# A diffusion backbone layer on one core: where the second halves of the normed tokens are made before an expert layer

## The chip, the core and the metric

One core of a Trainium2 chip runs the whole layer in one launch. The metric is the device time in microseconds (us). The engines named here are TensorE (PE, with its weight loads as PEld), VectorE (DVE), ScalarE (ACT), GpSimd (POOL) and SyncE (SP, which issues the loads from memory). Each engine works off its own instruction stream in order, and waits for others by semaphores.

## What is computed

The layer norms 512 latent tokens of width 1024, mixes them (neighbourhood attention and an RWKV-7 scan), projects and adds them to the residual, norms again, and sends each token to two of 32 experts. Everything of the change lies around the second norm, the router and the start of the expert layer:

```python
    yx = jnp.concatenate([na_x, rw_x], axis=-1) @ w_out
    x = x + mod_x[2] * yx
    hx2 = modulate(rmsnorm(x, norm2_g[l]), mod_x[3], mod_x[4])
    ...
    g_logits = (hf @ wg + bg).astype(jnp.float32)
    g_sel = jnp.argmax(g_logits, axis=-1)
    ...
    top_v, top_i = lax.top_k(e_logits, MOE_TOPK)
    ...
    for e in range(N_EXPERTS):
        he = jax.nn.silu(hf @ w1[e]) * (hf @ w3[e])
        out = out + combine[:, e:e + 1] * (he @ w2[e])
```

Inputs and weights are fp32. Each expert has three matrices of 2 MB (w1, w3, w2), so that the 32 experts read 201 MB.

## The kernel before

The 512 tokens lie in four tiles of 128 tokens, worked in the order 3, 2, 1, 0. `out_end` does the last of the output projection (`proj_rw`, whose accumulators are `acc`), the norm of each tile (`norm2`: transposes `pt`, sums of squares by ACT into `st`, a reciprocal root in small DVE steps into `rs`), and the router's logits (`logits`: `plg`, then `lt`, `plt` and `lg`). `best` finds the chosen experts of two tiles in some thirty small DVE instructions; its mask for the slots is `chosen`. `best(2)` serves tiles 3 and 2, `best(0)` tiles 1 and 0.

Tokens are gathered for the experts by matmuls with one-hot matrices (`oh2t` for tiles 3 and 2, `OH` afterwards), into PSUM tiles `pga`. The normed tokens come in two fp32r halves, so that the products keep fp32's precision: `xh` is x times its scale, rounded, made by ACT, and `xl` is what the rounding left, made by POOL out of an unrounded copy `xn` and `xh`. `halves` is a generator that makes both for one tile: one step makes `xh`, each further step a copy `xn` of 512 columns and its `xl`. For tiles 1 and 0 the copies lie in the room of the features `HS` instead of in `xn`. After the gather of batch 0 (experts 0 to 3), ACT scales `pga` into `HS`, and the experts' matmuls `ph` (w1 and w3) and `py` (w2) follow, two experts at a time.

The experts' weights are 384 loads of 512 KB, `wt`, all issued by SP in the order of use, and gathered in a ring of 31 tiles: `RING = (6, 15, 3, 3, 2, 2)` tiles in six pools, wt0 to wt5. The loads start long before the expert layer. A tile of the ring is memory that earlier work used, so its first load waits for the last reader there; from the 32nd on a load waits for the matmuls that used the tile before. wt1 and wt5 are allocated on the right side of memory, over the room of the pool `PR`, in which the router's small tiles (`lg`, `cwr`, `chosen`, `tsb`, then `xn`, then the tiles of `best`) lie one after the other. The SP queue is in order, so a load that waits holds back all behind it.

In `moe_phase`, `route_b` turns `chosen` into places (`byt`, line `s.pp[:, 0:2]`), two `slots` make the one-hot matrices `OH`, the rest of `best(0)` makes the weights of the chosen experts, and `route_c` writes the other places (the last `byt`, and the last reader of `chosen`). The scheduler orders an engine's stream except where code pins an instruction (`s.pin`) or an engine is kept in program order.

Of the kernel before, what the change touches and what calls it, by code (L numbers as in the profile page):

```python
# [8 lines left out]
F32 = mybir.dt.float32  # L9
# [3 lines left out]
AF = mybir.ActivationFunctionType  # L13
ALU = mybir.AluOpType
# [169 lines left out]
FIRST = ('k0', 'r0', 'v0')  # L184
ITEMS = (('k1', 'r1', 'v1', 'nk0'), ('k2', 'r2', 'v2', 'nq0'), ('k3', 'r3', 'v3', 'nv0'), ('nk1', 'gd', 'nq1', 'nv1'))  
MODGAP = 3.43  
H1 = (3, 2, 0)
UPE = lambda nc: nc.vector
LAST = 16  
OUT_ORD = ('scalar',)  # L190
# [35 lines left out]
class K:  # L226
# [1207 lines left out]
    def out_end(s, PCs):  # L1434

        nc, tc, ctx = s.nc, s.tc, s.ctx
        xt = s.MIX.tile([128, 8, 256], F32, name="xnt0", tag="mA")
        s.norm2(3, xt, 0, 'ch')
        acc = [[s.ps(tag=t, name="acc") for t in tt] for tt in (('ip', 'ip'), ('nt', 'rm'))]
        for n, _ in enumerate(s.proj_rw((1,), acc[0:1])):  # L1440
            if n == 3:
                s.norm2(2, xt, 1, 'ch')
        s.finish_b(0)
        lt = s.logits(xt, 'ch')
        PCs.close()
        s.BE.close()
        s.psc.close()
        ctx.enter_context(s.psum_pool("psg", g=2, m=2))
        PX = ctx.enter_context(tc.tile_pool(name="pxa", bufs=1, side="right", reuse_waits="tile"))
        s.xl, s.xh = [[PX.tile([128, 1024], F32R, name=f"{n}{i}") if i > 1 else None for i in range(4)] for n in ("xl", "xh")]  # L1450
        s.RT = ExitStack()
        s.PR = s.RT.enter_context(tc.tile_pool(name="pr", bufs=1, side="right", reuse_waits="tile"))
        s.lg = s.PR.tile([128, 4, 36], F32, name="lg")
        s.cwr = s.PR.tile([128, 2, 32], F32, name="cwr")
        s.chosen = s.PR.tile([128, 5, 32], BF16, name="chosen")
        nc.gpsimd.memset(s.chosen[:, 0], 0.0)

        s.tsb = s.PR.tile([128, 256], BF16, name="tsb")
        nc.gpsimd.tensor_copy(s.tsb, s.tsf)
        s.nio = s.L.tile([128, 32], F32, name="nio")  # L1460
        nc.gpsimd.tensor_copy(s.nio, s.niof)
        xt = s.MIX.tile([128, 8, 256], F32, name="xnt1", tag="mA")
        s.ordered = OUT_ORD
        for n, _ in enumerate(s.proj_rw((0,), acc[1:2])):
            if n == 1:
                s.logits_end((3, 2), lt)
                h = s.halves(3)
                s.some(h, 2)
            if n == 3:
                s.norm2(1, xt, 0)  # L1470
                s.some(h, 2)
        s.all(s.best(2))
        h = s.halves(2)
        s.some(h, 2)
        s.norm2(0, xt, 1)
        oh = s.route_a()
        lt = s.logits(xt)
        begun = s.begun = [s.ps((128, 2, 256), tag=g, name="pga") for g in ('rm', 'nt')]
        early = [(b, z, i) for b in range(4) for i in (3, 2) for z in range(2)]
        for b, z, i in early[:EARLY]:  # L1480
            s.gather_tiles(begun[b], oh, b, z, (i,))
        s.some(h, 2)
        s.logits_end((1, 0), lt)
        begun += [s.ps((128, 2, 256), tag='g', name="pga") for _ in range(2)]
        for b, z, i in early[EARLY:]:
            s.gather_tiles(begun[b], oh, b, z, (i,))

        s.mod5 = [s.ps(tag='m', name="mod5") for _ in range(2)]
        for m, c in zip(s.mod5, s.COLS):
            s.mm(m, s.cst[0:1, C_IOTA:C_IOTA + 1].to_broadcast([1, 128]), s.grow[:, c])  # L1490
        s.strict = False

    def norm2(s, i, xt, z, tag='m'):

        nc, PO = s.nc, s.PO
        st = PO.tile([128, 4], F32, name="st2", bufs=2)
        jk = PO.tile([128, 512], BF16, name="jk2", bufs=2)
        x = s.x1[:, i]
        for b in range(2):
            c = s.COLS[b]  # L1500
            pt = s.ps(tag=tag, name="pt2")
            for k in range(4):
                s.tr(pt[:, 128 * k:128 * k + 128], x[:, 512 * b + 128 * k:512 * b + 128 * k + 128])
            o = xt[:, 4 * b:4 * b + 4, 128 * z:128 * z + 128]
            p4 = pt.rearrange("p (a b) -> p a b", b=128)
            if b:
                nc.vector.tensor_copy(o, p4)
            else:
                s.act(o, p4)
            s.act(jk, x[:, c], AF.Square, accum_out=st[:, b:b + 1])  # L1510
        nc.vector.tensor_tensor(st[:, 1:2], st[:, 0:1], st[:, 1:2], ALU.add)
        nc.vector.tensor_scalar(st[:, 1:2], st[:, 1:2], 1.0 / D, EPS, op0=ALU.mult, op1=ALU.add)
        s.rsqrt(s.rs2[:, i:i + 1], st[:, 1:2], st[:, 3:4])

    def halves(s, i, room=None):

        rs = s.rs2[:, i:i + 1]
        s.act(s.xh[i], s.x1[:, i], AF.Copy, scale=rs)
        for c in s.COLS:
            yield  # L1520
            xn = room[:, c] if room is not None else s.PR.tile([128, 512], F32, name="xn")
            s.act(xn, s.x1[:, i, c], AF.Copy, scale=rs)
            s.pin(s.nc.gpsimd.tensor_tensor(s.xl[i][:, c], xn, s.xh[i][:, c].bitcast(F32), ALU.subtract))

# [16 lines left out]
    def moe_phase(s):  # L1541
        tc, nc = s.tc, s.nc
        with ExitStack() as es:
# [20 lines left out]
            OH, HS = PM.tile([128, 4, 4, 64], F32R, name="OH"), s.features_room(PM)  # L1564

            f = HS.rearrange("p k n -> p (k n)")
            h1, h0 = s.halves(1, f[:, 0:1024]), s.halves(0, f[:, 1024:2048])
            for h, n in ((h1, H1[0]), (h0, H1[1]), (h1, 3), (h0, H1[2])):
                s.some(h, n)
            s.pin(nc.gpsimd.tensor_copy(s.cw[:, 2:4], s.cwr))  # L1570
            best = s.best(0, h0)
            next(best)
            s.dump('lg', s.lg)
            s.dump('x1', s.x1)
            s.route_b()
            for i in (1, 0):
                s.pin(s.slots(OH[:, i], s.pp[:, i, 0:4]))
            s.all(best)
            s.ordered = ()
            s.route_c()  # L1580
# [36 lines left out]
        nc.vector.tensor_tensor(oh, it, bc(ix), ALU.is_equal)  # L1617
        yield

    def best(s, i0, more=()):  # L1620

        nc, PO = s.nc, s.PR
        T = lambda n, *sh: PO.tile([128, *sh], F32, name=n)
# [6 lines left out]
        t4, z, pg = T("t4", 2, 4), T("z", 2), T("pg", 2)  # L1630
# [26 lines left out]
        ex, w1, w2 = T("ex", 8), T("w1", 8), T("w2", 8)  # L1657
        nc.vector.tensor_tensor(ex, m2, m1, ALU.subtract)
        s.act(ex, ex, AF.Exp)
        s.all(more)  # L1660
        nc.vector.tensor_scalar(w1, ex, 1.0, None, op0=ALU.add)
        nc.vector.reciprocal(w1, w1)
        nc.vector.tensor_tensor(w1, w1, f8(t4), ALU.mult)
# [68 lines left out]
        return s.nc.vector.tensor_tensor(out, s.cst[:, None, C_IOTA:C_IOTA + 64].to_broadcast([128, 4, 64]),  # L1732
                                  place[:, :, None].to_broadcast([128, 4, 64]), ALU.is_equal)

    def gather_tiles(s, pg, OH, b, z, tiles):

        c = slice(256 * b + 128 * z, 256 * b + 128 * z + 128)
        for i in tiles:
            r = OH[i].rearrange("p e n -> p (e n)")
            s.mm(pg[:, z], s.xh[i][:, c], r, i == 3 and z == 0, False)  # L1740
            s.mm(pg[:, z], s.xl[i][:, c], r, False, i == 0 and z == 1)

    def gather(s, OH, HS, begun=None):
        nc = s.nc
        for b in range(4):
            pg = begun[b] if begun else s.ps((128, 2, 256), tag='gm'[b % 2], name="pga")
            for z in range(2):
                s.gather_tiles(pg, [OH[:, i] for i in range(4)], b, z, (1, 0) if begun else (3, 2, 1, 0))
                if z == 0:
                    yield  # L1750
            for z in range(2):
                kt = 2 * b + z
                s.act(HS[:, kt], pg[:, z], AF.Identity, scale=s.sc2[:, kt:kt + 1], bias=s.modv[:, kt:kt + 1])
            yield
# [240 lines left out]
```

## Time and profile before

| | |
|---|---|
| median of 3 runs | 1197.58 us (1192.83 to 1199.34) |
| the profiled execution's own time | 1196.86 us |
| its span | 1195.1 us |
| busy share of the span: PE, PEld, DVE, ACT, POOL | 91%, 64%, 56%, 34%, 21% |
| DMA | 310 MB, mean 259 GB/s |

The span is what the profiler saw from the first to the last instruction; the own time is 1.76 us longer. Times in the rows below count from the span's start. A busy PE is not PE at its peak, since matmuls are pipelined.

### The profile page before, as it was taken

What the parts mean: (1) busy time and instruction counts of PE and PEld (TensorE: products, weight loads), DVE (VectorE), ACT (ScalarE), POOL (GpSimd) and SP (SyncE); (2) the same over time, 40 slices, a digit from 0 to 9 for tenths busy, and PEclk for the clock granted to TensorE, in tenths of its full rate; (3) what the DMA queues carried; (4) which work ended last, traced back from release to release, by engine and by line L of the source; (5) the groups of instructions that cost most, each with busy time, mean ns of one, the idle gap of its engine ahead of it and who ended that gap; (6) DMA issues with size and microseconds to landing.
All of it is one profiled execution on the core that took longest, in us unless ns stands there. A gap on an engine that the chain in (4) does not pass through costs nothing.

```text
span 1195.1 us, 23927 instructions
## 1 busy us (share of the span) xinstructions
PE 1090.3 (91%) x9673; PEld 760.0 (64%) x9674; DVE 664.2 (56%) x1445; ACT 400.5 (34%) x759; POOL 247.4 (21%) x277
## 2 busy tenths in 40 slices
PE   3899987897977888999988979999999999999996
PEld 1677776775855767888776754646464646464644
DVE  5645598798699624554478772333333333333335
ACT  3543543634645444555322251111111111120200
POOL 0654463353344300020253030000000000000000
PEclk9999987797997888999999989999999999999998
DMA  9534643545554477764353939999999999999995
GB/s 367 177 133 144 197 147 119 155 138 154 160 171 126 133 202 211 241 158 108 103 151 117 359 124 372 409 408 409 408 409 409 409 409 409 408 409 409 408 409 188
DMA packets 148765, 310.00 MB, mean 259 GB/s; under 512 B 32291, under 2 KB 71075, under 8 KB 148652
## 3 DMA queue, kind: packets, MB, share of 16 engines
q1 hardware_dynamic: 143868, 306.08, 71.9%
q10 hardware_dynamic: 4752, 2.36, 0.7%
q8 instruction: 77, 1.26, 0.4%
q14 instruction: 36, 0.29, 0.1%
q0 software_dynamic: 32, 0.00, 0.0%
HBM read 283.22 MB, written 25.17 MB: 258 GB/s over the span
## 4 chain that ended last, share of the span: by engine, by line
PE 55%; DVE 16%; DMA 6%; ACT 2%; issue 1%; POOL 1%; SPq 0%; DVEq 0%; POOLq 0%; ACTq 0%
PE ph L241 16%; PE py L241 9%; PE psc L241 7%; PE pga L241 5%; DMA wt<-in_w_dram 3%; DVE Tc L211 3%; DVE tmp L211 3%; PE pgr L241 3%; PE ipn L241 3%; PE pr L241 1%; PE ppt L245 1%; PE pon L241 1%; DVE fst L211 1%; DMA BKj<-BKd 1%; PE acc L241 1%
## 5 line engine op out<-in xcount | busy, mean ns | idle before, releaser
L241 PE MATMUL ph<-wt,HS 128*64 128x512 f32 x1024 | 224.5, 593 | 0.2 <-DMA wt<-in_w_dram 0.2
L241 PEld LDWEIGHTS ph<-wt,HS 128*64 128x64 f32 x1024 | 73.5, 137 | 140.5 <-issue 126.7
L211 DVE TENSOR_TENSOR hid<-hid,ph 128x512 f32<-128x512 f32 x16 | 11.0, 688 | 249.2 <-PE ph L241 249.2
L241 PE MATMUL py<-wt,hid 128*64 128x256 f32 x1024 | 114.5, 381 | 0.0
L241 PEld LDWEIGHTS py<-wt,hid 128*64 128x64 f32 x1024 | 71.9, 137 | 40.3 <-issue 3.9
L211 POOL CAST two<-sel 128x128 fp32r<-128x128 f32 x32 | 8.5, 293 | 425.3 <-PE pbc L241 425.3
L241 PE MATMUL ipn<-whi,hth 128*128 128x256 f32 x256 | 80.3, 314 | 15.8 <-DVE vs L211 15.3
L211 POOL TENSOR_TENSOR wlo<-wraw,whi 128x512 fp32r<-128x512 f32 x54 | 73.8, 1369 | 77.6 <-ACT whi L211 74.5
L211 DVE TENSOR_TENSOR x<-psc,x 128x512 f32<-128x512 f32 (+1 forms) x136 | 78.5, 648 | 0.0
L241 PE MATMUL ip<-hth,whi 128*128 128x512 f32 (+1 forms) x200 | 75.8, 379 | 1.9 <-ACT nr L211 1.9
L241 PE MATMUL ipn<-wlo,hth 128*128 128x256 f32 x256 | 75.6, 295 | 0.0
L241 PE MATMUL ipn<-whi,htl 128*128 128x256 f32 x256 | 75.4, 295 | 0.0
L241 PE MATMUL ip<-htl,whi 128*128 128x512 f32 (+1 forms) x200 | 72.2, 361 | 0.7 <-DVE htl L211 0.7
L241 PE MATMUL ip<-hth,wlo 128*128 128x512 f32 (+1 forms) x200 | 71.9, 359 | 0.0
L241 PEld LDWEIGHTS ipn<-whi,hth 128*128 128x128 f32 x256 | 51.9, 203 | 24.6 <-issue 22.1
L241 PE MATMUL pga<-OH,xh 128*128 128x256 f32 x240 | 60.0, 291 | 0.9 <-DVE OH L211 0.9
L211 DVE TENSOR_TENSOR Tc<-Tc,tmp 128x30 f32<-128x30 f32 (+14 forms) x120 | 59.4, 495 | 2.0
L211 DVE TENSOR_TENSOR tmp<-Mc,Tc 128x30 f32<-128x30 f32 (+14 forms) x120 | 57.7, 481 | 3.1 <-ACT Tc L211 1.1
L241 PE MATMUL pga<-OH,xl 128*128 128x256 f32 x240 | 59.0, 287 | 0.0
L241 PE MATMUL psc<-yh,oht 128*128 128x512 f32 (+1 forms) x136 | 54.5, 405 | 1.2 <-DVE x L211 0.8
L211 ACT ACTIVATE hid<-pth 128x512 f32<-128x512 f32 x16 | 9.6, 598 | 133.1 <-PE pth L245 133.1
L241 PEld LDWEIGHTS ipn<-whi,htl 128*128 128x128 f32 x256 | 52.3, 204 | 0.0
(352 smaller groups left out, 2252.6 us busy)
## 6 DMA issues: line engine op xcount, KB each, us to landing
wt<-in_w_dram SPq DMA_DIRECT2D x384, 512.0 KB
wm<-in_wmod_dram SPq DMA_DIRECT2D x48, 512.0 KB
wraw<-in_w_in_dram SPq DMA_DIRECT2D x30, 256.0 KB
wraw<-in_w_na_dram SPq DMA_DIRECT2D x24, 256.0 KB
BKj<-BKd SPq DMA_DIRECT2D x12, 512.0 KB
BKd<-BK SPq DMA_DIRECT2D x12, 384.0 KB
ARz<-ARd SPq DMA_DIRECT2D x16, 256.0 KB
wo<-in_w_out_dram SPq DMA_DIRECT2D x16, 256.0 KB
```

The lines of the kernel that those rows point to most:

```text
L211: i = f(*a, **k)
L241: i = s.nc.tensor.matmul(out, l, r, start=start, stop=stop)
L245: i = s.nc.tensor.transpose(out, x, s.ident if ident is None else ident)
```

## The change

It does four things. `halves` of tiles 3 and 2 run through at once, ahead of the norms of tiles 1 and 0, and `xn` gets two buffers (`XN = 2`). `halves` of tiles 1 and 0 make only `xh` and one whole copy early; their `xl` are four DVE subtractions behind the first two `OH`. Batch 0 gathers the `xh` of tiles 1 and 0 first and their `xl` last. In `norm2` the sum of squares stands ahead of the copy of the transposed tokens.

```diff
-H1 = (3, 2, 0)
+XN = 2
...
             if n == 1:
                 s.logits_end((3, 2), lt)
-                h = s.halves(3)
-                s.some(h, 2)
+                s.all(s.halves(3))
+            if n == 2:
+                s.all(s.halves(2))
             if n == 3:
                 s.norm2(1, xt, 0)
-                s.some(h, 2)
         s.all(s.best(2))
-        h = s.halves(2)
-        s.some(h, 2)
         s.norm2(0, xt, 1)
...
+            s.act(jk, x[:, c], AF.Square, accum_out=st[:, b:b + 1])
             if b:
                 nc.vector.tensor_copy(o, p4)
             else:
                 s.act(o, p4)
-            s.act(jk, x[:, c], AF.Square, accum_out=st[:, b:b + 1])
...
         s.act(s.xh[i], s.x1[:, i], AF.Copy, scale=rs)
+        if room is not None:
+            s.act(room, s.x1[:, i], AF.Copy, scale=rs)
+            yield
         for c in s.COLS:
+            if room is not None:
+                s.pin(s.nc.vector.tensor_tensor(s.xl[i][:, c], room[:, c], s.xh[i][:, c].bitcast(F32), ALU.subtract))
+                continue
             yield
-            xn = room[:, c] if room is not None else s.PR.tile([128, 512], F32, name="xn")
+            xn = s.PR.tile([128, 512], F32, name="xn", bufs=XN)
...
-            for h, n in ((h1, H1[0]), (h0, H1[1]), (h1, 3), (h0, H1[2])):
-                s.some(h, n)
+            for h in (h1, h0):
+                next(h)
...
             for i in (1, 0):
                 s.pin(s.slots(OH[:, i], s.pp[:, i, 0:4]))
+            for h in (h1, h0):
+                s.all(h)
             s.all(best)
...
+        if begun:
+
+            for b in range(4):
+                for z in range(2):
+                    s.gather_tiles(begun[b], [OH[:, i] for i in range(4)], b, z, (1, 0), (0,))
         for b in range(4):
...
-                s.gather_tiles(pg, [OH[:, i] for i in range(4)], b, z, (1, 0) if begun else (3, 2, 1, 0))
+                s.gather_tiles(pg, [OH[:, i] for i in range(4)], b, z, (1, 0) if begun else (3, 2, 1, 0), (1,) if begun else (0, 1))
```

SP's queue from the 20th to the 31st weight load, in the kernel before (the names in brackets are the engines waited for; DMAHW is an earlier load's end):

```order
L211 DMA wt1_8464<-in_w2_dram 128x1024 [waits DMAHW0_49]
L211 DMA wt1_8466<-in_w2_dram 128x1024 [waits DMAHW1_49]
L211 DMA wt2_8468<-in_w2_dram 128x1024 [waits DMAHW2_49,Pool_49]
L211 DMA wt2_8470<-in_w2_dram 128x1024 [waits DMAHW3_49,DVE_49]
L211 DMA wt2_8472<-in_w2_dram 128x1024 [waits DMAHW4_49,DVE_49]
L211 DMA wt3_8550<-in_w1_dram 128x1024 [waits DMAHW5_49,PE_49]
L211 DMA wt3_8552<-in_w1_dram 128x1024 [waits DMAHW6_49]
L211 DMA wt3_8558<-in_w1_dram 128x1024 [waits DMAHW7_49]
L211 DMA wt4_8560<-in_w1_dram 128x1024 [waits DVE_49,DMAHW0_49,PE_49,Activation_49]
L211 DMA wt4_8566<-in_w1_dram 128x1024 [waits DMAHW1_49]
L211 DMA wt5_8568<-in_w1_dram 128x1024 [waits DVE_49,PE_49,DMAHW2_49,Activation_49,Pool_49]
L211 DMA wt5_8574<-in_w1_dram 128x1024 [waits DMAHW3_49,Activation_49]
```

The same queue in the changed kernel, from the 19th to the 25th load:

```order
L211 DMA wt1_8460<-in_w2_dram 128x1024 [waits DMAHW7_49]
L211 DMA wt1_8462<-in_w2_dram 128x1024 [waits DMAHW0_49]
L211 DMA wt1_8464<-in_w2_dram 128x1024 [waits DVE_49,DMAHW1_49,PE_49,Pool_49]
L211 DMA wt2_8466<-in_w2_dram 128x1024 [waits DMAHW2_49]
L211 DMA wt2_8468<-in_w2_dram 128x1024 [waits DMAHW3_49]
L211 DMA wt2_8470<-in_w2_dram 128x1024 [waits DMAHW4_49]
L211 DMA wt3_8548<-in_w1_dram 128x1024 [waits DMAHW5_49]
```

The wait for DVE, PE and POOL that the 30th load had (wt5_8568) stands at the 21st (wt1_8464): both name the count that DVE reaches with the last `byt` of `route_c`. With a second `xn` of 2 KB in a partition, `chosen` begins 2 KB lower than before, and so lies under the last tile of wt1 instead of under wt5.

DVE's stream behind the first two one-hot matrices, as a piece of the difference (xl1 and xl0 are the second halves of tiles 1 and 0):

```order
+L211 TENSOR_TENSOR OH_8261<-cst_66,byt_8249 128x256 x2
+L211 TENSOR_TENSOR xl1_8246<-HS_8262,xh1_8248 128x512 x2
+L211 TENSOR_TENSOR xl0_8245<-HS_8262,xh0_8247 128x512
+L211 TENSOR_REDUCE z_8278<-t4_8277 128x2
+L211 TENSOR_TENSOR xl0_8245<-HS_8262,xh0_8247 128x512
+L211 RECIPROCAL pg_8279<-z_8278 128x2
+L211 TENSOR_SCALAR w1_8320<-ex_8319 128x8
```

Four instructions of 512 columns now stand between the `OH` and the rest of `best(0)`, which ends with the last `byt`.

ACT's stream from the first rounded half of tile 3 on, as a piece of the difference:

```order
 L211 ACTIVATE xh3_7994<-x1_5023,rs2_6964 128x1024
 L211 ACTIVATE xn_8019<-x1_5023,rs2_6964 128x512
-L211 ACTIVATE xnt1_8006<-pt2_8030 128x4x128
-L211 ACTIVATE jk2_8029,st2_8028<-x1_5023 128x512 x2
-L211 ACTIVATE xn_8057<-x1_5023,rs2_6964 128x512
-L211 ACTIVATE t4_8083<-t4_8083 128x8
-L211 ACTIVATE ex_8115<-ex_8115 128x8
+L211 ACTIVATE xn_8022<-x1_5023,rs2_6964 128x512
 L211 ACTIVATE xh2_7993<-x1_5023,rs2_6964 128x1024
```

The second copy of tile 3 and the halves of tile 2 move ahead of tile 1's norm, and with them POOL's subtractions.

## Rows read from the trace of the kernel before

**Rows 1.** Page, loads by tile: issuing queue, operation, count, KB of each.

```profile
wt<-in_w_dram SPq DMA_DIRECT2D x384, 512.0 KB
```

**Rows 2.** Busy time by stretch; the last columns are granted clock, DMA share, GB/s.

```profile
651.00:684.00 33.00, 31.33 (x347) 25.00 (x346) 26.13 (x83) 7.77 (x17) 0.46 (x2) 1.00 0.96 381
684.00:703.00 19.00, 15.12 (x100) 12.01 (x99) 15.79 (x70) 12.92 (x25) 8.66 (x11) 1.00 0.40 142
703.00:712.00 9.00, 5.12 (x22) 3.66 (x21) 8.17 (x37) 2.84 (x7) 3.16 (x5) 0.69 0.00 0
712.00:717.00 5.00, 5.00 (x32) 3.73 (x33) 0.58 (x4) 3.95 (x9) 0.67 (x1) 0.87 0.66 210
717.00:723.00 6.00, 6.00 (x32) 2.00 (x30) 0.00 (x0) 1.60 (x2) 0.00 (x0) 1.00 0.71 211
723.00:1171.00 448.00, 447.04 (x2729) 247.32 (x2726) 162.98 (x265) 66.02 (x117) 7.96 (x30) 1.00 1.03 409
1171.00:1176.00 5.00, 5.00 (x36) 3.43 (x37) 4.86 (x9) 0.60 (x1) 0.00 (x0) 1.00 0.56 223
```

**Rows 3.** The chain that ended last: start, length, engine and tile.

```profile
709.52 5.73 PE pga L241 x32
...
1119.38 7.82 PE pga L241 x64
...
1156.34 10.18 DMA wt<-in_w_dram
1166.56 1.94 PE ph L241 x6
```

**Rows 4.** Waits of SP's queue, 684 to 724 us: total, times, longest.

```profile
SPq L211 <- DVE byt L211: 13.3, 1, 13.3
```

**Rows 5.** Timeline of SP's queue at two loads' issue: start, length.

```profile
711.39 0.80 SPq L211 DMA_DIRECT2D wt<-in_w_dram  x2
...
717.14 0.33 SPq L211 DMA_DIRECT2D wt<-in_w_dram  x1
```

**Rows 6.** Busy time in the stretch behind the second of these.

```profile
717.00:721.00 4.00, 4.00 (x22) 1.38 (x20) 0.00 (x0) 1.01 (x1) 0.00 (x0) 1.00 0.68 220
```

**Rows 7.** Timeline of POOL: subtractions, one and two in a row.

```profile
686.26 1.29 POOL L211 TENSOR_TENSOR xl<-xn,xh 128x512 fp32r<-128x512 f32 x1 [3.51 <-ACT xn L211]
...
700.48 2.54 POOL L211 TENSOR_TENSOR xl<-HS,xh 128x512 fp32r<-128x512 f32 x2
```

**Rows 8.** Timeline of DVE, from the router's first choice to its last.

```profile
688.32 0.15 DVE L211 TENSOR_REDUCE gi<-gc 128x2 f32<-128x8 f32 x1
...
691.31 1.29 DVE L211 TENSOR_TENSOR chosen<-es,ohg 128x64 bf16<-128x64 f32 x1
...
698.39 1.15 DVE L211 SCALAR_TENSOR_TENSOR rs<-st,rs 128x1 f32<-128x1 f32 x1
...
699.96 0.16 DVE L211 SCALAR_TENSOR_TENSOR rs<-st,rs 128x1 f32<-128x1 f32 x1
...
700.58 1.19 DVE L211 SCALAR_TENSOR_TENSOR rs<-st,rs 128x1 f32<-128x1 f32 x1
...
701.89 0.26 DVE L211 SCALAR_TENSOR_TENSOR lg<-plt,rs,browb 128x36 f32<-128x36 f32 x1
702.27 0.79 DVE L211 COPY el<-lg 128x64 f32<-128x64 f32 x1
...
703.31 0.16 DVE L211 TENSOR_TENSOR t<-lg,gm 128x8 f32<-128x8 f32 x1
...
704.03 0.97 DVE L211 TENSOR_TENSOR ohg<-nio,gi 128x8 f32<-128x8 f32 x1
...
706.98 1.29 DVE L211 TENSOR_TENSOR chosen<-es,ohg 128x64 bf16<-128x64 f32 x1
```

**Rows 9.** Timeline of DVE: a subtraction of 512 columns, and the last byt.

```profile
582.90 0.68 DVE L211 TENSOR_TENSOR wol<-wo,woh 128x512 fp32r<-128x512 f32 x1
...
711.03 0.21 DVE L211 SCALAR_TENSOR_TENSOR byt<-ppos,chosen 128x64 f32<-128x64 f32 x1
```

More of the change, by code (lines that the diff above doesn't have):

```diff
@@ L1481, in out_end @@
             s.gather_tiles(begun[b], oh, b, z, (i,))
-        s.some(h, 2)
         s.logits_end((1, 0), lt)
@@ L1567, in moe_phase @@
             h1, h0 = s.halves(1, f[:, 0:1024]), s.halves(0, f[:, 1024:2048])
-            for h, n in ((h1, H1[0]), (h0, H1[1]), (h1, 3), (h0, H1[2])):
-                s.some(h, n)
+            for h in (h1, h0):
+                next(h)
             s.pin(nc.gpsimd.tensor_copy(s.cw[:, 2:4], s.cwr))
-            best = s.best(0, h0)
+            best = s.best(0)
             next(best)
@@ L1618, in first_max, with best @@
         yield
-    def best(s, i0, more=()):
+    def best(s, i0):
         nc, PO = s.nc, s.PR
@@ L1659, in best @@
         s.act(ex, ex, AF.Exp)
-        s.all(more)
         nc.vector.tensor_scalar(w1, ex, 1.0, None, op0=ALU.add)
@@ L1733, in slots, with gather_tiles @@
                                   place[:, :, None].to_broadcast([128, 4, 64]), ALU.is_equal)
-    def gather_tiles(s, pg, OH, b, z, tiles):
+    def gather_tiles(s, pg, OH, b, z, tiles, parts=(0, 1)):
         c = slice(256 * b + 128 * z, 256 * b + 128 * z + 128)
@@ L1739, in gather_tiles @@
             r = OH[i].rearrange("p e n -> p (e n)")
-            s.mm(pg[:, z], s.xh[i][:, c], r, i == 3 and z == 0, False)
-            s.mm(pg[:, z], s.xl[i][:, c], r, False, i == 0 and z == 1)
+            for x in parts:
+                s.mm(pg[:, z], (s.xl if x else s.xh)[i][:, c], r, i == 3 and z == x == 0, i == 0 and z == x == 1)
     def gather(s, OH, HS, begun=None):
         nc = s.nc
+        if begun:
+            for b in range(4):
+                for z in range(2):
+                    s.gather_tiles(begun[b], [OH[:, i] for i in range(4)], b, z, (1, 0), (0,))
         for b in range(4):
```

## The prediction

> **What bounds the kernel now.** I read the busy time by stretch first, because it shows the weight stream and TensorE side by side. From 723 us to 1171 us the DMA share is 1.03 and the rate 409 GB/s in one unbroken stretch, while TensorE is busy for 447.04 of 448 us [rows 2]. Two resources are full at once, so the next view is the chain that ended last: it shows which of them sets the end. Most of the expert phase it goes through TensorE, but its last part before the final matmuls goes through the loads: links of 10.18 us of wt up to 1166.56 us, then the last six `ph` [rows 3]. The reader is to see that the stream comes in just behind TensorE at the end. A later stream therefore moves the end one for one; an earlier TensorE alone moves nothing.
>
> So the question is when the stream becomes unbroken. A tile has 512 KB [rows 1], 0.524 MB. By stretch [rows 2] there landed 33.00 us x 381 GB/s = 24.0 tiles up to 684 us, 5.1 up to 703 us, none up to 712 us, 2.0 up to 717 us and 2.4 up to 723 us: 33.5 by 723 us. After 1171 us 5.00 x 223 GB/s = 2.1 tiles are left. The stretch between carried 384 - 33.5 - 2.1 = 348.4 tiles in 448 us, 1.286 us for one. The holes before 723 us are waits of SP's queue: the longest for DVE is one of 13.3 us for `byt` [rows 4], and it ends with the issue at 711.39 us [rows 5], right behind the last `byt` (711.03 + 0.21 us) [rows 9]. That is the 30th load in the order of the queue.
>
> **The change part by part.** *The second `xn`.* By the order shown above, the wait for the last `byt` moves from the 30th load to the 21st. Loads 21 to 31 then come behind that `byt` instead of two of them. No work hides this: the stream has no free time behind 723 us in which to catch up. With B for the issue behind `byt` and L for the time from an issue to full rate, the stream has 384 - 20 - 2.1 = 361.9 tiles to bring from B + L on, against 348.4 from 723 us on. The end moves by 13.5 x 1.286 - (723 - B - L), that is 17.4 us less what the stream starts ahead of 723 us. L from the rows: issue at 717.14 us [rows 5], and 4.00 us x 220 GB/s = 1.68 tiles, 2.16 us at full rate, by 721 us [rows 6]; so L = 721 - 2.16 - 717.14 = 1.7 us. With B unchanged at 711.39 us this alone is 17.4 - 9.9 = +7.5 us. The end stays where it is only if B falls to 703.9 us.
>
> The price of a tile is checked against a page. The Trainium skill's "DMA: Bandwidth & Descriptors", section "Where 436 GB/s comes from", says that about 358 GB/s is what binds loads from HBM; a tile would then take 1.46 us and the whole sum below would be +10.1 us. The trace has 409 GB/s over 448 us, and I take the trace.
>
> *B: the four POOL subtractions of tiles 3 and 2.* They now follow each other without a break, since ACT makes their copies in a row: from 686.26 us, four of 1.29 us (two in a row take 2.54 us, so no gap) [rows 7], up to 691.4 us. While POOL subtracts, a DVE instruction with two operands in SBUF stands still: `rs` takes 1.15 and 1.19 us where the same step takes 0.16 us, and the second of them ends at 701.77 us, as the first POOL subtraction of that pair does (700.48 + 1.27) [rows 7, 8]. Before, `best(2)` runs between two subtractions; now nearly all of it falls under the four. I let one instruction through at each of their ends, which leaves `gi` and all behind it: 691.31 - 688.32 = 3.0 us, and 0.2 us for `chosen` itself (128x64, as the last `byt` with 0.21 us [rows 9]). `best(2)`'s `chosen` ends at 691.4 + 3.2 = 694.6 us instead of 692.6 us: +2.0 us. Behind it on DVE queue tile 0's two residual additions, for which TensorE's transposes wait.
>
> *B: the subtractions that POOL no longer makes.* From that `chosen` to the second `lg` were 701.89 - 692.60 = 9.3 us, with the two held `rs` in them; 1.0 us each goes, leaving 7.3. The `lg` stays at 701.9 us. From `lg` to the end of `best(0)`'s `chosen` were 6.4 us; `el` (0.79 for 0.2), `ohg` (0.97 for 0.16) and `chosen` (1.29 for 0.2) give back 0.6 + 0.8 + 1.1 = 2.5 us [rows 8]. `chosen` ends at 705.8 us instead of 708.3 us.
>
> *B: the four subtractions on DVE.* One of this form takes 0.68 us [rows 9], so 2.7 us stand between `OH` and the rest of `best(0)`. From `chosen` to the last `byt` were 711.24 - 708.27 = 3.0 us; now 5.7 us. The `byt` ends at 711.5 us, SP issues 0.15 us later: B = 711.6 us. What the shorter chain gave, the subtractions take back.
>
> *Gather and `norm2`.* The gather starts 2.5 us earlier, at 707.0 us. Its 32 matmuls take 5.73 us [rows 3], the 16 with `xh` half of that; the first `xl` of both tiles are there 2.1 us behind `OH`, so these 16 cover them. If TensorE ran at full clock, 16 would take 2.0 us (64 take 7.82 us [rows 3]), and it would wait some 0.5 us for the last. Neither matters, since the stream is last. The square ahead of the copy is the same work in another order: nothing.
>
> The sum: 17.4 - (723 - 711.6 - 1.7) = **+7.7 us**. Against the execution's own time, 1196.86 us (1.76 us around its span of 1195.1 us), that is 1204.6 us; the median of the runs shown is 0.7 us above it, 1205.3 us. I give 1205.0 us.
>
> **Rivals.** *The held DVE.* If `best(2)` is not held, the 2.0 us go: B = 709.6 us, +5.7 us, 1202.6 us. For it speaks that a DVE instruction which starts first might make POOL wait instead; against it that POOL's rows keep 1.29 us and DVE's grow. The Trainium skill's "SBUF — State Buffer", section "Who interferes with whom", says just this: the pair of ports goes for the whole instruction to whichever issues first, and the other waits. By that rule DVE and POOL could take turns here; no row shows POOL losing.
>
> *The clock.* TensorE waits 2.0 us longer now between the projection and tile 0's transposes. In 684 to 703 us it stood still for 3.9 of 19.00 us and kept a granted clock of 1.00; in 703 to 712 us it stood still for as long, 3.9 of 9.00 us, and this stretch and the next had 0.69 and 0.87 [rows 2], a spell at the lower level (1.2 of 2.4 GHz). Such a spell before `lg` would slow 16 logits and 12 gathers: 5.73/32 - 7.82/64 = 0.057 us each [rows 3], 1.6 us in all. B = 713.2 us, +9.3 us, 1206.2 us.
>
> *Not slower.* If the end is TensorE's and not the stream's, the wait at the 21st load costs nothing and the 2.5 us of the gather are won: 1194.4 us. It decides if B is below 703.9 us, or if the stream has 8 us in hand at the end. Against it stand the load links at the end of the chain [rows 3] and the share of 1.03 [rows 2].
>
> **How the numbers follow.** The sum as it stands 0.60, the clock 0.18, the held DVE 0.14, not slower 0.08. Half a per cent, 6 us, is about what a measurement of this kernel can tell. Slower by more: 0.55 of the first, 0.18, and 0.05 of the third, 0.78. Within: 0.05, 0.09 and 0.05 of the last, 0.19. Faster: 0.03. The range reaches from below the unheld case to above the clock's and leaves out the last: 1201 to 1209 us.
>
> **What would show it.** Right: the DMA rate is nothing from about 679 us (the 20th tile, four tiles before 684 us) to 713 us; SP waits more than 30 us once, for `byt`; POOL subtracts without a break from 686 to 691 us and never afterwards; TensorE waits for loads well before the links of 1156 us. Wrong: loads land between 690 and 702 us as before, or TensorE does not wait more than now at the end.

## The result, and the profile after

| | before | changed |
|---|---|---|
| median, device us | 1196.88 (6 runs, 1192.32 to 1199.34) | 1205.77 (6 runs, 1201.90 to 1208.53) |
| span of the profiled execution | 1195.1 | 1204.0 |
| issue of the load behind the last `byt` (B) | 711.39 | 711.96 |

The changed kernel is slower: the ratio is 1.0072, 95% interval [1.0046, 1.0098], +8.9 us between the medians. The forecast was 1205.0 us, slower.

Busy time by stretch of the changed kernel, in the stretches of [rows 2] and with their columns (length; busy time and number of instructions of PE, PEld, DVE, ACT and POOL; granted clock, DMA share, GB/s):

```profile
651.00:684.00 33.00, 31.34 (x336) 24.92 (x333) 25.60 (x82) 8.16 (x19) 0.46 (x2) 1.00 0.81 319
684.00:703.00 19.00, 14.50 (x87) 11.22 (x87) 15.29 (x72) 11.82 (x22) 6.56 (x10) 0.91 0.00 1
703.00:712.00 9.00, 8.11 (x45) 6.50 (x44) 7.88 (x38) 3.00 (x7) 0.19 (x1) 0.83 0.00 1
712.00:717.00 5.00, 5.00 (x29) 2.58 (x30) 1.15 (x5) 3.54 (x8) 0.78 (x2) 0.97 0.75 274
717.00:723.00 6.00, 6.00 (x32) 2.00 (x30) 0.00 (x0) 1.88 (x2) 0.00 (x0) 1.00 0.95 330
723.00:1171.00 448.00, 445.20 (x2689) 244.87 (x2687) 160.65 (x261) 66.01 (x117) 7.96 (x30) 1.00 1.03 409
1171.00:1176.00 5.00, 4.59 (x20) 1.21 (x17) 0.00 (x0) 0.00 (x0) 0.00 (x0) 1.00 1.03 409
```

The last two columns tell it. Up to 684 us 20.1 tiles land instead of 24.0, then nothing up to 712 us, where before 5.1 landed. The rate behind 723 us is the same 409 GB/s, so nothing is caught up, and the stream still runs at full rate from 1171 to 1176 us, where it was ending before. SP's longest wait between 660 and 724 us (total, times, longest), and the issue behind it, from the timeline (start, length):

```profile
SPq L211 <- DVE byt L211: 41.9, 1, 41.9
```
```profile
711.96 0.33 SPq L211 DMA_DIRECT2D wt<-in_w_dram  x1
```

One wait of 41.9 us for `byt` stands where 13.3 us stood [rows 4]. The chain that ended last goes through the loads from 886.82 us on. Before, it came to them, but for one load at 722.29 us, at 1135.93 us, two links ahead of the one in [rows 3]. The kernel before, then the changed one:

```profile
1135.93 10.18 DMA wt<-in_w_dram
```

```profile
880.98 5.83 PE pga L241 x48
886.82 10.18 DMA wt<-in_w_dram
...
1165.30 10.17 DMA wt<-in_w_dram
1175.51 1.95 PE ph L241 x6
```

TensorE now waits for the stream in the middle of the expert phase too. How B came about is seen on POOL, DVE and TensorE; the rows answer to [rows 7 to 9]. POOL:

```profile
685.71 5.09 POOL L211 TENSOR_TENSOR xl<-xn,xh 128x512 fp32r<-128x512 f32 x4 [21.39 <-ACT xn L211]
```

DVE, held under it, then free:

```profile
687.24 1.06 DVE L211 TENSOR_TENSOR gc<-lg,gm 128x8 f32<-128x8 f32 x1
688.22 1.34 DVE L211 TENSOR_TENSOR t<-lg,gm 128x8 f32<-128x8 f32 x1
689.48 1.41 DVE L211 TENSOR_TENSOR ac<-el,m 128x64 f32<-128x64 f32 x1
690.81 0.15 DVE L211 TENSOR_TENSOR gc<-gc,nio 128x8 f32<-128x8 f32 x1
...
694.05 0.23 DVE L211 TENSOR_TENSOR chosen<-es,ohg 128x64 bf16<-128x64 f32 x1
...
702.28 0.26 DVE L211 SCALAR_TENSOR_TENSOR lg<-plt,rs,browb 128x36 f32<-128x36 f32 x1 [0.44 <-PE plt L241]
...
705.92 0.23 DVE L211 TENSOR_TENSOR chosen<-es,ohg 128x64 bf16<-128x64 f32 x1
...
707.80 1.89 DVE L211 TENSOR_TENSOR xl<-HS,xh 128x512 fp32r<-128x512 f32 x3
...
709.67 0.68 DVE L211 TENSOR_TENSOR xl<-HS,xh 128x512 fp32r<-128x512 f32 x1
...
711.60 0.22 DVE L211 SCALAR_TENSOR_TENSOR byt<-ppos,chosen 128x64 f32<-128x64 f32 x1
```

TensorE, from the projection's last matmul (the first line of each piece) to the logits, of the kernel before and then of the changed one:

```profile
691.28 0.39 PE L241 MATMUL acc<-woh,mixl 128*128 128x512 f32 x1
693.61 1.22 PE L245 MATMUL pt<-cst,x 128*128 128x128 f32 x8 [1.94 <-DVE rs L211]
...
694.92 2.17 PE L241 MATMUL plg<-xnt,wgs 128*64 128x256 f32 x16
```
```profile
690.74 0.39 PE L241 MATMUL acc<-woh,mixl 128*128 128x512 f32 x1
694.93 1.85 PE L245 MATMUL pt<-cst,x 128*128 128x128 f32 x8 [3.81 <-DVE x L211]
...
696.95 2.75 PE L241 MATMUL plg<-xnt,wgs 128*64 128x256 f32 x16
```

These two pieces also give a landmark. TensorE's work up to the projection's end is the same in all kernels here, yet it ends at 691.67 us in one execution, at 691.13 us in the next, and between 687.7 and 696.9 us in the runs below. The scatter arises ahead of the router's first `lg`, which starts 5.8 us ahead of the landmark in all twelve traces; it is in the medians too. Measured from the landmark, four kernels with the same wait and nearly the same B (the changed one, e6, e7, e8) end within 0.2 us of each other, though their spans lie 8.9 us apart. One execution of each kernel was traced. From the landmark to the end of the span it is 503.4 us before (1195.1 - 691.67) and 512.8 us in the changed kernel: +9.4 us. B is 19.7 us behind the landmark before, 20.8 us in the changed kernel.

### The profile page after: what moved, and what is told of

The parts are those of the page before. It is cut to its first block, busy times and chain, and to the rows that moved or that the text cites. A ratio compares the mean times of both kernels' runs of the same rounds, so it can differ in the third digit from the quotient of the medians.

```text
span 1204.0 us, 23923 instructions
## 1 busy us (share of the span) xinstructions
PE 1106.3 (92%) x9673; PEld 767.6 (64%) x9674; DVE 663.2 (55%) x1449; ACT 400.2 (33%) x757; POOL 241.3 (20%) x273
## 4 chain that ended last, share of the span: by engine, by line
PE 40%; DMA 21%; DVE 15%; ACT 2%; issue 1%; POOL 1%; SPq 0%; ACTq 0%; DVEq 0%; POOLq 0%
DMA wt<-in_w_dram 20%; PE ph L241 8%; PE psc L241 5%; PE py L241 5%; PE pga L241 3%; DVE Tc L211 3%; DVE tmp L211 3%; PE ipn L241 2%; PE pgr L241 2%; PE pr L241 2%; PE ppt L245 1%; PE pon L241 1%; DVE fst L211 1%; DVE oacc L211 1%; PE acc L241 1%
## 5 line engine op out<-in xcount | busy, mean ns | idle before, releaser
L241 PE MATMUL ph<-wt,HS 128*64 128x512 f32 x1024 | 233.0, 595 | 2.5 <-DMA wt<-in_w_dram 2.3
L211 DVE TENSOR_TENSOR Tc<-Tc,tmp 128x30 f32<-128x30 f32 (+14 forms) x120 | 63.3, 527 | 2.0
L241 PE MATMUL pga<-OH,xl 128*128 128x256 f32 x240 | 56.5, 286 | 0.0
```

The source lines that it names most:

```text
L211: i = f(*a, **k)
L241: i = s.nc.tensor.matmul(out, l, r, start=start, stop=stop)
```

## The experiments

Theory: the second `xn` pushes `chosen` under the 21st load, and every load held behind the last `byt` costs the stream one tile. Rivals: the new order of POOL's and DVE's work costs it; or TensorE's gather sets the end. Times from the landmark (projection's end), in us, of one profiled execution each:

| run | median (before in the same call) | ratio, 95% interval | B | `ph` starts | end | end against before |
|---|---|---|---|---|---|---|
| before | | | 19.7 | 23.5 | 503.4 | |
| changed | 1205.77 (1196.88) | 1.0072 [1.0046, 1.0098] | 20.8 | 22.3 | 512.8 | +9.4 |
| e1, one `xn` | 1194.49 (1195.52) | 0.9986 [0.9967, 1.0005] | 20.1 | 21.5 | 502.2 | -1.2 |
| e2, before, two `xn` | 1204.94 (1195.52) | 1.0084 [1.0058, 1.0111] | 19.4 | 23.4 | 511.8 | +8.3 |
| e3, before, sixteen | 1212.14 (1195.52) | 1.0133 [1.0110, 1.0157] | 21.0 | 24.6 | 521.7 | +18.3 |
| e4, `xn` first | 1195.17 (1195.52) | 0.9994 [0.9973, 1.0016] | 20.7 | 22.1 | 502.3 | -1.1 |
| e5, rest first | 1202.34 (1196.26) | 1.0055 [1.0030, 1.0079] | 18.5 | 22.7 | 510.1 | +6.6 |
| e6, silu early | 1205.20 (1196.26) | 1.0084 [1.0052, 1.0115] | 21.1 | 22.5 | 512.8 | +9.3 |
| e7, counts late | 1204.12 (1196.26) | 1.0070 [1.0044, 1.0096] | 20.7 | 22.2 | 513.0 | +9.5 |
| e8, filler of 14 | 1202.51, one run | | 20.9 | 20.9 | 513.0 | +9.5 |
| e9, combination | 1194.15 (1195.93) | 0.9983 [0.9963, 1.0003] | 19.2 | 20.6 | 500.4 | -3.1 |
| e10, and rest first | 1192.81 (1195.93) | 0.9982 [0.9965, 0.9998] | 17.9 | 21.7 | 501.7 | -1.7 |

**e1: one buffer.**

```diff
-XN = 2
+XN = 1
```

> The changed kernel with one buffer for xn; every stream but DVE's is the same word for word, and on DVE a few neighbours change places. The wait of SP's queue for the last byt stands at the 30th weight load again, as in the kernel before. Theory (the memory of the second xn is what costs): the loads 21 to 29 land early again, and the two behind the last byt, issued at about 711.9 us, are no later than before by more than 0.5 us; ph starts about 1.8 us earlier than in the kernel before (713.4 for 715.2 us), the 32nd load waits for it and is issued 1.8 us earlier, and the end follows: 1.8 us less than the kernel before, about 1195 us, 10.5 us less than the changed kernel. Rival (the order of POOL's and DVE's work costs it, through a later byt and TensorE's waits): it stays at 1204 to 1206 us.

SP's wait and two stretches of this run:

```profile
SPq L211 <- DVE byt L211: 11.2, 1, 11.2
```
```profile
684.00:703.00 19.00, 15.26 (x92) 11.07 (x90) 16.28 (x85) 12.69 (x25) 5.57 (x9) 0.91 0.40 138
703.00:712.00 9.00, 8.49 (x46) 6.52 (x48) 5.82 (x22) 3.81 (x9) 0.96 (x2) 0.81 0.35 115
```

The loads land early again (138 GB/s up to 703 us) and the whole loss is gone. All the rest of the change, with its held DVE and its spells at the lower clock, is worth -1.2 us from the landmark; by the medians it is not told from no change.

**e2 and e3: only room, in the kernel before.** The five streams are unchanged.

```diff
-            xn = room[:, c] if room is not None else s.PR.tile([128, 512], F32, name="xn")
+            xn = room[:, c] if room is not None else s.PR.tile([128, 512], F32, name="xn", bufs=2)
```

(e3: `bufs=16`.)

> The kernel before with two buffers for xn and nothing else: all five streams are the same word for word, and only the addresses move, so that the wait for the last byt stands at the 21st weight load. Theory (memory alone): the last byt is at 711.0 us as before, and the end moves by 13.5 tiles of 1.286 us less 9.9 us, +7.5 us: 1204.4 us against a median of 1196.9 us. Rival (the order costs it): no change, or 1 us better, since a second buffer frees ACT from a wait for POOL.

> The kernel before with sixteen buffers for xn (only five copies are ever made; the rest is room): again the same streams word for word. The wait for the last byt moves from the 30th to the 14th weight load. Theory: every load that the wait comes earlier costs one tile of the stream, 1.286 us: 7 more than with two buffers, 13.5 + 7 = 20.5 tiles, 26.4 - 9.9 = +16.5 us, 1213.4 us. Rival (the stream has some slack, or fills faster behind a long hole): clearly less than that, at or below +12 us. Rival (order): no change.

SP's wait for `byt`, e2 and then e3:

```profile
SPq L211 <- DVE byt L211: 40.6, 1, 40.6
```
```profile
SPq L211 <- DVE byt L211: 49.8, 1, 49.8
```

2 KB of room in a partition alone cost what the change cost, +9.4 us by the medians (+8.3 us from the landmark), and 30 KB cost +16.6 us (+18.3 us, of which 1.3 us is B). The dose goes with the number of loads behind the wait: 7 loads more at 1.286 us are 9.0 us; measured are 7.2 us by the medians, and 9.9 us from the landmark, 8.4 us once the later B (1.55 us) is taken off. Neither rival asks for any of this.

**e4: two buffers, laid down first.**

```diff
+        s.xq = [s.PR.tile([128, 512], F32, name=f"xq{k}") for k in range(2)]
         s.lg = s.PR.tile([128, 4, 36], F32, name="lg")
...
-            xn = s.PR.tile([128, 512], F32, name="xn", bufs=XN)
+            xn = s.xq[c.start // 512]
```

> The changed kernel with both buffers of xn kept, but laid down first in the pool, ahead of lg, cwr and chosen; the order of ACT, POOL and SP is the same. Under the last tile of wt1 then lies the first xn, whose last reader is the third POOL subtraction in a row, at about 689.5 us, and chosen lies under wt5 again. Theory: the 21st load waits to about 690 us and no further, the queue catches up before the 30th, which waits for the last byt at 711.9 us, and the time is that of the run with one buffer, about 1195 us (at most 2 us more, if the loads held up to 690 us do not all land before). Rival (a second buffer costs by what it does to the order, not by where it lies): 1204 to 1206 us.

```profile
SPq L211 <- POOL xl L211: 18.7, 1, 18.7
SPq L211 <- DVE byt L211: 11.2, 1, 11.2
```

The same memory and the same order cost nothing once the tile that is read last lies under the load that is issued last. The 18.7 us at the 21st load are free, since the queue catches up before the 30th.

**e5: B alone.** `s.all(best)` and `s.route_c()` stand ahead of the loop over `h1, h0`:

```diff
+            s.all(best)
+            s.route_c()
             for h in (h1, h0):
                 s.all(h)
-            s.all(best)
             s.ordered = ()
-            s.route_c()
```

> The changed kernel (two buffers, wait at the 21st load) with the rest of best(0) and route_c ahead of the four DVE subtractions. Theory (the end follows B, the issue behind the last byt, one for one): the last byt ends 2.55 us earlier (1.89 + 0.68 us in the changed kernel's timeline), the 21st load is issued at about 709.4 us instead of 711.96 us, and the end comes 2.5 us earlier, about 1203 us beside 1205.8 us for the changed kernel in its runs; the gather of the xl halves waits about 1 us for the later subtractions, which the late stream hides. Rival (TensorE's gather sets the end): 1206 us or more, since ph starts later.

B falls by 2.3 us and the end by 2.8 us, although `ph` starts 0.5 us later than in the changed kernel. The ratio falls from 1.0072 to 1.0055, with intervals that overlap. In this trace the end follows the stream, not the gather.

**e6 and e7: the hole behind the burst.** The stream isn't at full rate at once. Two stretches of the changed kernel, and POOL's transfer of the counts ahead of them:

```profile
720.00:721.00 1.00, 1.00 (x8) 0.31 (x6) 0.00 (x0) 0.99 (x2) 0.00 (x0) 1.00 0.75 74
721.00:722.00 1.00, 1.00 (x6) 0.29 (x4) 0.00 (x0) 0.20 (x1) 0.00 (x0) 1.00 0.69 246
```
```profile
713.12 0.67 POOL L211 DMA_DIRECT2D cntd<-hid  x1 [1.01 <-DVE hid L211]
```

Issued loads wait there while the DMA engines move 74 GB/s. e6 puts ACT's table load early; e7 delays the transfer.

```diff
             s.all(best)
+            s.act(m5[:, 0:1], s.cst[:, 0:1], AF.Silu)
```
```diff
-        cnt = PM.tile([128, 512], F32, name="hid")[:, 0:33]
+        cnt = s.cnt = PM.tile([128, 33], F32, name="cnt")
...
-        s.pin(nc.gpsimd.dma_start(s.cntd, cnt[0:1, 0:32]))
...
+                if e == 4:
+                    s.pin(nc.gpsimd.dma_start(s.cntd, s.cnt[0:1, 0:32]))
```

> The changed kernel with one more ACT instruction (a silu of one column, into a place that is overwritten afterwards) behind the last Exp, so that the table load of ACT stands at about 705.5 us, while no weight load is in flight, instead of 719.31 us. In the changed kernel the DMA engines stand still from about 719.9 to 721.3 us although six loads are issued, and the 33rd load is issued 2.62 us behind the 32nd, where 1.28 us is the pace from then on. Theory A (the table load takes the DMA queues' time): the hole goes, the 33rd load comes 1.3 us behind the 32nd, and the end is 1.3 us earlier, about 1204.5 us. Rival B (the hole comes from the transfer of cntd, or from the queue itself): the hole stays within 0.5 us of its place, and the time is that of the changed kernel.

> The changed kernel with the transfer of the counts (cntd, 0.1 KB, issued by POOL at 713.12 us and landed 6.1 us later) moved behind the first two pairs of experts, from a tile of its own, so that the first hid no longer waits for it. Theory B (this transfer is what leaves the hole at 720 us): the hole goes, the 33rd load comes 1.3 us behind the 32nd, and the end is 1.3 us earlier, about 1204.5 us; a hole would show again where cntd now stands. Rival A (ACT's table load): the hole comes earlier with the table load, which now waits for ph alone (about 716 us). Rival C (the queue itself, behind a burst of ten issues): the hole stays at 720 us.

e6, the table load, the transfer, and the stretch with the hole:

```profile
711.15 1.28 ACT L211 ACT_TABLE_LOAD   x1
```
```profile
719.10 0.67 POOL L211 DMA_DIRECT2D cntd<-hid  x1 [1.01 <-DVE hid L211]
```
```profile
726.00:727.00 1.00, 1.00 (x8) 0.29 (x5) 0.00 (x0) 0.47 (x1) 0.00 (x0) 1.00 0.97 111
```

e7, the transfer and three stretches:

```profile
729.44 0.67 POOL L211 DMA_DIRECT2D cntd<-cnt  x1
```
```profile
717.00:723.00 6.00, 6.00 (x31) 2.01 (x28) 0.00 (x0) 0.60 (x1) 0.00 (x0) 1.00 1.03 410
...
737.00:738.00 1.00, 1.00 (x8) 0.36 (x6) 0.67 (x1) 0.30 (x1) 0.00 (x0) 1.00 0.71 279
```

Theory A falls: with the table load 14 us earlier, counted from the landmark, and so ahead of all these loads, the hole stays, 7.2 us behind the transfer's issue. Theory B holds for e7: without the transfer the stream runs at 410 GB/s through 717 to 723 us, and a smaller hole stands at 737 us, 7.3 us behind the new issue. From issue to hole it is 6.9 to 7.3 us, read in steps of 0.25 us, in six of the seven kernels with an early wait; in e3 there is only a shallow dip. But the transfer alone does not bring a hole. In e9 it is issued late into the running stream, which then keeps 407 GB/s for 12 us:

```profile
1143.57 0.67 POOL L211 DMA_DIRECT2D cntd<-cnt  x1
```
```profile
1144.00:1156.00 12.00, 12.00 (x88) 5.98 (x86) 4.76 (x7) 1.26 (x2) 0.24 (x1) 1.00 1.03 407
```

In e10, with the same late transfer, the stream only dips, to 315 GB/s in 1148 to 1149 us, 6.6 to 7.6 us behind the issue at 1141.43 us.

Theory B's expected gain of 1.3 us is not seen: the end from the landmark is unchanged, and by the medians of the same call e7 is 1.1 us under e6, with intervals that overlap. What the hole needs beside the transfer, and what it costs at the end, stays open.

**e8: TensorE kept busy.**

```diff
+        dm = s.ps(tag='m', name="dm")
+        for n in range(14):
+            s.mm(dm, s.xh[3][:, 0:128], s.xh[3][:, 0:512], n == 0, n == 13)
         s.norm2(0, xt, 1)
```

> The changed kernel with 14 matmuls of 512 columns on TensorE (about 0.23 us each, 3.2 us) between the projection and tile 0's transposes, where it stood still for 3.8 us; their result is read by nobody. Theory (the spell at the lower clock from about 695.4 to 698.7 us follows from standing still): the granted clock stays at 1.00 in 684 to 703 us (0.91 in the changed kernel), the 16 logit matmuls take about 1.5 us instead of 2.75 us, and the last byt ends 1.0 to 1.5 us earlier, B at about 710.7 us. Rival (the spell has another cause): 0.91 and 2.75 us stay, B at 711.9 us or later.

```profile
689.94 3.46 PE L241 MATMUL dm<-xh 128*128 128x512 f32 x14 [2.15 <-DVE bc L211]
693.24 1.03 PE L245 MATMUL pt<-cst,x 128*128 128x128 f32 x8
...
704.47 2.37 PE L241 MATMUL pga<-OH,xh 128*128 128x256 f32 x16 [0.89 <-DVE OH L211]
706.67 2.08 PE L241 MATMUL pga<-OH,xl 128*128 128x256 f32 x16
```

The clock is 1.00 from 684 to 712 us, the transposes take 1.03 instead of 1.85 us, the logits 1.95 instead of 2.75 us, the gather 4.3 us. That part holds. The forecast for B missed: the fillers waited 2.15 us for DVE (by the code for a PSUM buffer that DVE was still reading, which no row shows by itself) and ended some 1.6 us too late, which took back what the clock gave (B 20.9 us from the landmark). And `ph` starts 1.4 us earlier than in the changed kernel while the end stays, which speaks once more for the stream.

**e9 and e10: a version meant to beat both.** One `xn`, 6 fillers, the transfer of the counts behind the last pair of experts; e10 with e5's edit as well.

> The changed kernel with one buffer for xn, with 6 instead of 14 filler matmuls on TensorE ahead of tile 0's transposes (14 lasted from 689.94 to 693.4 us, 1.65 us past the gap; 6 end about 691.4 us), and with the transfer of the counts (cntd) behind the last pair of experts. Theory: the wait stands at the 30th load; both spells at the lower clock go (1.00 in 684 to 703 us and in 703 to 712 us; the transposes take 1.03 instead of 1.85 us, the 16 logit matmuls 1.95 instead of 2.75 us, the gather 4.2 instead of 5.7 us), so that ph and the 32nd load come 2.5 to 3 us earlier than in the run with one buffer alone; no hole some 7.4 us behind cntd's issue, another 0.6 to 1.3 us. The end: 2.5 to 4 us less than with one buffer alone (1194.5 us), 1190.5 to 1192 us, 0.4% under the kernel before. Rival (TensorE, busy for 447 of 448 us in the expert phase, sets the end once the stream starts earlier): no more than 1 us under 1194.5 us.

> The same, and the rest of best(0) and route_c ahead of the four DVE subtractions, so that the 30th and 31st loads are issued 2.5 us earlier. Theory: the 32nd load waits for ph, whose gather now waits 0.8 us for the later subtractions; the two loads landing earlier leave a hole up to the 32nd that is as long as what they gained. No difference beyond 1 us from the run before this one. Rival (B decides here as it does with the wait at the 21st load): 2.5 us less.

e9, two stretches:

```profile
684.00:703.00 19.00, 16.28 (x105) 12.85 (x104) 15.55 (x80) 13.46 (x24) 6.57 (x10) 1.00 0.39 142
703.00:712.00 9.00, 8.11 (x44) 6.50 (x43) 7.81 (x32) 2.74 (x8) 0.29 (x1) 0.81 0.03 5
```

The first spell went, the second did not (0.81), so `ph` came only 0.9 us earlier than in e1. From the landmark e9 ends 1.9 us ahead of e1 and 3.1 us ahead of the kernel before; expected were 2.5 to 4 us against e1, and no more than 1 us by the rival: between the two. What each of its three parts gave is not separated. By the medians the three versions with one `xn` can't be told apart. e10 ends 1.4 us behind e9, a little more than the 1 us that was expected at most: its first spell came back (0.91 in 684 to 703 us), and its earlier 30th and 31st loads gave nothing. By the medians e10 is 1.3 us ahead of e9, less than their scatter. Both lie about 1% under the changed kernel; under the kernel before by 0.2%, e9 with an interval that holds 1, e10 with one that just leaves it out. A gain of e9 over the kernel before is not shown, and one of e10 only just.

## Why the prediction was right

**The wait at the 21st load**: right, and it is the whole loss (e1, e2, e4). Its bound, that no later stretch catches up, held: 409 GB/s again.

**+7.5 us with B unchanged**: e2 is this term by itself. By its own B, 0.3 us earlier, it should give +7.2 us; measured from the landmark are +8.3 us. The term was some 1.1 us short: it let the stream run at full rate from B + L on, but in the changed kernel 717 to 723 us had 330 of 409 GB/s, 1.2 us lost (79/409 x 6 us), to the hole behind the counts' transfer. That this hole is the 1.1 us is argued, not shown: by its own B e7, with no hole there and a smaller one later, still ends some 1 us behind the term, and e3, with a dip alone, some 0.5 us. L itself fitted: 274 GB/s x 5 us are 2.6 tiles by 717 us, as many as 711.96 + 1.7 us and 1.286 us a tile give.

**B, 711.6 us forecast**: 711.96 us measured, but that execution runs 0.5 us ahead of the one before, so B is 20.8 us from the landmark for a forecast of 19.9 us (711.6 - 691.67). Term by term: `best(2)` held, +2.0 us forecast, +2.2 us measured (`chosen` ends 3.15 us from the landmark for 0.94 us). `chosen` to the second `lg`, 7.3 us forecast, 8.0 us measured: this is the one that missed. `lg` to `chosen`, 3.9 us forecast (6.4 - 2.5), 3.87 us measured. `chosen` to the last `byt`, 5.7 us both.

**The clock**: the spell of the rival given 0.18 came. TensorE stood still for 3.81 us ahead of the transposes, a spell at 1.2 GHz followed (0.91 in 684 to 703 us), and transposes and logits took 0.6 us longer each. `lg` came 0.9 us later than forecast, 0.2 us of it with `best(2)`, where the rival had 1.6 us. The gather's spell came as well (0.83 in 703 to 712 us), under the stream. e8 shows the cause in part: with most of the stillness filled, no spell. But the longer pause is not the whole cause. e3 stood still no longer than the kernel before, and its transposes ran at the lower level:

```profile
696.76 1.86 PE L245 MATMUL pt<-cst,x 128*128 128x128 f32 x8 [1.91 <-DVE rs L211]
```

Its clock was 0.91 in 684 to 703 us, where the kernel before, behind 1.94 us, had 1.00; e9 and e10 both stood still for 1.75 us at this place, and had 1.00 and 0.91. What decides it is open.

**The held DVE**: held, so the rival with DVE not held falls. DVE's `gc`, `t` and `ac` took 1.06, 1.34 and 1.41 us, one let through per subtraction, and POOL's four took 1.27 us each. The Trainium skill's "SBUF — State Buffer", section "Who interferes with whom", lets whoever issues first hold the shared ports for a whole instruction; these rows agree for DVE waiting on POOL, and no row shows the reverse.

**Not slower**: falls by e5 and e8, where the gather comes later or earlier and the end goes with B.

**An earlier TensorE alone moves nothing**: right in the changed kernel (e8), wrong where the wait stands at the 30th load. There the 32nd load waits for `ph`: it is issued 1.96 us behind its start in the kernel before and in e1, e4, e9 and e10. From that start to the end these five take 479.8 to 480.7 us, the other seven 487.3 to 497.1 us. So there the gather sets when the stream becomes unbroken, and e9, with `ph` 2.9 us earlier, ends 3.1 us earlier than the kernel before. Nor are the two resources equally full. A batch of four experts, 48 loads, takes TensorE 59.15 us where it does not wait, as these links of the chain before show; 48 tiles of the stream take 61.7 us (48 x 1.286):

```profile
772.32 13.88 PE ph L241 x64
...
831.47 13.88 PE ph L241 x64
```

TensorE gains on the stream through the phase and catches up with it near the end, which a busy share of 447.04 in 448 us does not tell.

**The sum**: 7.7 us forecast and 0.9 us of later B make 8.6 us; 9.4 us are measured from the landmark, 8.9 us by the medians. The last 0.8 us is open; the hole's 1.2 us would more than fill it. That the forecast of 1205.0 us lies 0.8 us from the median is in part luck: from the landmark the sum was 1.7 us short, and single runs scatter by more. The price of a tile stood at the 409 GB/s of the rows. By the 358 GB/s of the Trainium skill's "DMA: Bandwidth & Descriptors", section "Where 436 GB/s comes from", the sum would have been +10.1 us, an estimate; the trace does not agree with that rate, and with the later B this sum would overshoot.

## What to carry to other kernels

When a scratch tile grows, list what lies under each later load and who reads it last: 2 KB of scratch in a partition moved one wait by nine loads of an in-order queue and cost 9 us in a kernel whose instructions had not changed. Lay the tiles that are read last under the loads that are issued last. And measure against a landmark in the same trace that the change can't touch: the runs of one kernel scatter by 4 to 13 us here, and differences of about 1 us could still be read.

## What was not expected of the hardware

A transfer of 0.1 KB issued by POOL was followed, 6.9 to 7.3 us behind its issue, by a hole in a 409 GB/s stream from another queue (about 1.2 us of the stream in the changed kernel, less in e7), in six of the seven kernels with an early wait. It moved with the transfer and not with ACT's table load, but behind the same transfer in e9 there was none, and in e3 and e10 a dip. And the granted clock in 684 to 703 us did not follow the pause ahead of the transposes alone: 0.91 behind 3.81 us, 1.00 behind 2.15 us (e8, ahead of the fillers), 1.00 behind 1.94 us before and 0.91 behind 1.91 us in e3, and 1.00 and 0.91 behind the same 1.75 us in e9 and e10.
